# A hand-made order for TensorE in the RWKV stage of a decoder layer

## The chip, the cores and the metric

The kernel runs on one core of a Trainium2 chip. The metric is the device time of one execution in microseconds (us), input to output, and lower is better. One execution was recorded by the hardware profiler; all rows below are from it.

## The reference, cut to what matters

One layer of a decoder, for a prompt of 1024 tokens and 8 sample tokens (1032 columns together). The normed input is projected once, by a wide matrix; the columns of that projection are an RWKV branch, a sliding-window attention, a cross attention and three gates of 1024 columns each:

```python
h = _rmsnorm(x, p['norm_mix'])
proj = h @ p['w_in']
z, q, k, v, xq, gates = jnp.split(proj, IN_SPLITS, axis=-1)
...
out_a, S_new = _rwkv_branch(z, z_prev, S0, p)
...
g = jax.nn.sigmoid(gates)
merged = (g[..., :D_MODEL] * (out_a @ p['w_br_a'])
          + g[..., D_MODEL:2 * D_MODEL] * (out_b @ p['w_br_b'])
          + g[..., 2 * D_MODEL:] * (out_c @ p['w_br_c']))
x = x + merged @ p['w_out']
```

The RWKV branch has 8 heads of 64 and is a recurrence over the tokens, with a state matrix for each head:

```python
sa = jnp.einsum('bhvk,bhk->bhv', S, -kk_t)
S = (S * w_t[:, :, None, :] + sa[..., None] * (kk_t * a_t)[:, :, None, :]
     + v_t[..., None] * k_t[:, :, None, :])
y = jnp.einsum('bhvk,bhk->bhv', S, r_t)
```

The vectors `kk` are normed to length one for each head; `y` is normed, scaled, and multiplied by an output gate.

## The kernel before, in words

**The input projection** is done in pieces of 128 of its columns (`in_proj`): a load of 512 KB (`wst`), a split of the weights into two parts (`wh` on ScalarE, `wl` on GpSimd), and 72 products on TensorE: three column groups (384, 384 and 264 of the 1032 tokens) by 8 blocks of the depth by 3 pairs of parts (L181 to L183, in `dense`). ScalarE then evacuates each group. A gate piece ends in a tanh and a store (L286, L287); an RWKV piece ends in the token shift on VectorE (L348 to L350). There are 48 pieces.

**The RWKV stage** handles the recurrence in 8 units: two groups of four heads by four quarters of the 1024 tokens. Unit u does, in this order:

- first half: loads of z; the decay and `aa` products (L459, L460); a scan (L470); sums of squares by products with `hsel` (L481), an inverse root of some ten small VectorE operations (L122 to L127), L493 and L496, a second `hsel` product (L498); a transpose of the norms, written to memory and read back over all partitions (`bsum`, then `rn`, L506 and L510), for `kk` times `rn` (L512); then `BR` and `CK` (L536 to L539).
- the matrices: 32 products of `CK` and `BR` (L548), masked into `GM` on VectorE (L551). The 32 by 32 diagonal blocks go out to memory (`amat<-GM`, L555) and come back in another layout (`AT<-amat`, L577).
- the loop on VectorE: 31 steps of two operations (L584, L586) solve the small triangular systems. The result goes out (`xmat<-X`, L588) and into `GM` (`GM<-xmat`, L591); a transpose (L593) follows.
- the two inverse steps on TensorE: 16 products (L600) with an evacuation by ScalarE, and 16 more (L603).
- four chunks one after the other, each a chain: state times `BR` (L618), `GM` times `UV` (L627), ScalarE (L630), a product (L634), ScalarE (L635), a product (L637), the new state on VectorE (L640); L642 makes the output of the chunk.
- the end: group norm on VectorE (L660, L661) and ScalarE (L669), transposes (L672), the output gate's products (L680), a store.

The state goes from unit to unit within a group of heads, so chunks of different units of a group can't change places. The pools hold two buffers of `GM`, `BR`, `CKT` and `UV`, one of `AT`.

**What sets the order.** The program is written unit by unit, with pieces of the input projection between (a list `FILL`: RWKV pieces of the second group, and ten gates). A scheduler then orders the instructions of each engine. In what it made, the matrices of unit u + 1 (L548) stand on TensorE ahead of the inverse steps of unit u (L600), and the loop of unit u + 1 on VectorE lies between the state updates (L640) of unit u. Twenty-two pieces lie in the stage; the last four gates are made where the branches are merged, just before the branch projections.

Of the kernel before, what the change touches and what calls it, by code (L numbers as in the profile page):

```python
# [18 lines left out]
P = 128  # L19
# [70 lines left out]
def tile_step(ctx, tc, I, O):  # L90
    nc = tc.nc
    V, A, G, PE, SY = nc.vector, nc.scalar, nc.gpsimd, nc.tensor, nc.sync
    cnt = [0]

# [181 lines left out]

    gate_d = mk(dr, "gate", [24, P, NT])
    todo = list(range(24))

    def gates(n):  # L280
        for _ in range(min(n, len(todo))):
            i = todo.pop(0)

            def evac(g, s, w, b):
                gt = mk(hp, "gt", [P, w], F32, 2)
                op = A.activation(gt, b, AF.Tanh, scale=0.5)  # L286
                SY.dma_start(gate_d[i, :, s:s + w], gt)  # L287
                return op
            in_proj(G0 + i * P, evac)
# [50 lines left out]
    def rw_proj(mt, out):  # L340
# [6 lines left out]
        G.tensor_copy(zl[:, :, mt], z[:, T:T + 9])  # L347
        V.tensor_tensor(out[:, 0:T], z[:, 0:T], z[:, 1:T + 1], ALU.subtract)  # L348
        V.tensor_tensor(out[:, T:NT], shT[:, :, mt], z[:, T + 1:NT + 1], ALU.subtract)
        V.scalar_tensor_tensor(out, out, col(C_MU + mt), z[:, 1:NT + 1], ALU.mult, ALU.add)  # L350
# [80 lines left out]
    def unit(jj, q):  # L431
# [56 lines left out]
        rsqrt(sn[:, 0], sn[:, 2], sn[:, 1])  # L488
        for e in range(2):
# [4 lines left out]
        for e in range(2):  # L494
            for c in spans[e]:
                V.scalar_tensor_tensor(tmp[:, c], zr[:, c], col(C_RK + 2 * jj + e), zk[:, c], ALU.mult, ALU.mult)  # L496
        for i, (c0, w) in enumerate(tl):
            PE.matmul(sb[:w, 1, :, i], lhsT=tmp[:, c0:c0 + w], rhs=hsel, start=True, stop=True)  # L498
        V.tensor_copy(sn[:, 3, :, 0:4], sb[:, 1, :, 0:4])
        if end:  # L500
            V.tensor_copy(sn[0:2 * NS, 3, :, 4], sb[0:2 * NS, 1, :, 4])
        b = sm_bank([20, P])
# [40 lines left out]
        for c4 in range(2):  # L543
# [13 lines left out]
        for x in range(2):  # L557
            xs_ = slice(4 * x, 4 * x + 4)
            G.tensor_tensor(CK[:, xs_].rearrange("p c a t -> p c (a t)"), CK[:, xs_].rearrange("p c a t -> p c (a t)"),
                            gc[:, xs_].unsqueeze(2).to_broadcast([P, 4, P]), ALU.mult)  # L560
        CKT, UV = mk(rp, "CKT", [P, HN, P], F32, 2), mk(rp, "UV", [P, HN, P], F32, 2)
        for x in range(2):
# [3 lines left out]
            A.activation(CKT[:, 4 * x:4 * x + 4], b, AF.Copy)  # L566
        b = sm_bank([P, 4, P])
        for i in range(4):
            PE.transpose(b[:, i], zv[:, i * P:(i + 1) * P], ident)
        for par in range(2):  # L570
            A.activation(UV[64:128].rearrange("p (c e) v -> p c e v", e=2)[:, :, par], b[par * 64:par * 64 + 64], AF.Copy)

# [21 lines left out]
        XP = mk(rp, "Y", [32, 16, 32])  # L594
        for x in range(2):
# [17 lines left out]
        for cc in range(4):  # L613
# [16 lines left out]
            A.activation(pt, pp[0:64], AF.Copy)  # L630
            pz = cp_bank([P, 512])
# [3 lines left out]
            A.activation(UVc[0:64, :, cc], pu, AF.Copy)  # L635
            for e, hh, hs in both:
# [7 lines left out]
            A.activation(Yc[(cc % 2) * 64:(cc % 2) * 64 + 64, :, cc // 2], pp[64:128], AF.Copy)  # L644
        if end:
# [24 lines left out]
        b = cp_bank([P, 4, P])  # L670
# [6 lines left out]
        for s, w, cols in banks:  # L677
            b = cp_bank([P, w])
# [1100 lines left out]
```

## Time and profile before

| what | value |
| --- | --- |
| time, median of 3 runs | 2063.13 us (2058.52 to 2069.75) |
| the profiled execution's own time | 2070.15 us |
| its span, first to last instruction | 2068.2 us |
| TensorE busy | 1928.9 us (93%) |
| VectorE, ScalarE, GpSimd busy | 63%, 38%, 31% |
| TensorE's granted clock over the span | 0.946 of full speed |
| the RWKV stage | 182 to 730 us, TensorE's clock 0.81 to 1.00 by unit |

The profiled execution took 7.0 us more than the median. "Busy" adds up the time of an engine's instructions; a wait inside the pipeline of matrix products also counts as busy.

### The profile page before, as it was taken

Reading aid. Unit: us, or ns where it says so; the run is one execution under the profiler, and the core shown is the slowest. Engines: PE = TensorE matmul, PEld = TensorE weight load, DVE = VectorE, ACT = ScalarE, POOL = GpSimd, SP = SyncE. Lnnn points to the kernel's source line nnn. Section 1 sums busy time; section 2 is a strip of 40 time slices with the busy share of each in tenths; the row PEclk is TensorE's granted clock in tenths of the full one; section 3 lists DMA queues with packets and bytes.
Section 4 is the critical chain, followed back from the end, with each engine's and each line's share of the span. In section 5 each row is a group of like instructions: output and inputs, shape, how many; then the busy total and the mean of one; then the engine's idle time right before and its main releaser. Section 6 shows DMA issues by size and latency. Waiting matters only on the chain. (4 is left out here: it accounts for less than half of the span.)

```text
span 2068.2 us, 36968 instructions
## 1 busy us (share of the span) xinstructions
PE 1928.9 (93%) x14079; PEld 1835.2 (89%) x14079; DVE 1305.7 (63%) x3021; ACT 786.1 (38%) x1701; POOL 643.8 (31%) x706
## 2 busy tenths in 40 slices
PE   5998889989999988999999999979999998999998
PEld 4878777878888978989889999969999998999997
DVE  7545756465565466467742575687665668788864
ACT  5432323433433334345642123343333344344433
POOL 3423212322321144222010000146755644444321
PEclk9999888989999999989989999979999999999999
DMA  4543322333321155233236346416444448455413
GB/s 142 168 156 115 98 52 78 94 93 81 96 81 52 37 160 163 62 92 89 67 114 197 113 144 199 123 43 203 155 149 144 147 151 277 124 149 156 142 39 101
DMA packets 257102, 250.68 MB, mean 121 GB/s; under 512 B 43101, under 2 KB 204958, under 8 KB 256926
## 3 DMA queue, kind: packets, MB, share of 16 engines
q1 hardware_dynamic: 254656, 241.24, 38.3%
q0 software_dynamic: 2016, 6.53, 1.0%
q8 instruction: 111, 1.82, 0.4%
q10 hardware_dynamic: 254, 0.55, 0.1%
q14 instruction: 65, 0.53, 0.1%
HBM read 174.19 MB, written 74.46 MB: 120 GB/s over the span
## 5 line engine op out<-in xcount | busy, mean ns | idle before, releaser
L181 PE MATMUL mm<-hh,wh 128*128 128x384 f32 (+1 forms) x1152 | 390.0, 339 | 5.3 <-ACT z L345 5.0
L182 PE MATMUL mm<-hl,wh 128*128 128x384 f32 (+1 forms) x1152 | 386.9, 336 | 6.9 <-DVE hl L217 6.9
L183 PE MATMUL mm<-hh,wl 128*128 128x384 f32 (+1 forms) x1152 | 384.8, 334 | 1.4 <-POOL wl L174 1.4
L1566 PE MATMUL z<-h,wl 128*128 128x258 f32 x1488 | 266.6, 288 | 10.1 <-ACT wh L1547 3.4
L1566 PE MATMUL z<-h,wh 128*128 128x258 f32 x1488 | 264.8, 286 | 6.6 <-DVE wh L1321 3.6
L182 PEld LDWEIGHTS mm<-hl,wh 128*128 128x128 f32 x1152 | 225.6, 196 | 10.9 <-DVE hl L217 7.7
L181 PEld LDWEIGHTS mm<-hh,wh 128*128 128x128 f32 x1152 | 225.1, 195 | 9.4 <-ACT z L345 5.4
L1566 PEld LDWEIGHTS z<-h,wl 128*128 128x128 f32 x1488 | 218.3, 193 | 12.0 <-ACT wh L1547 3.5
L183 PEld LDWEIGHTS mm<-hh,wl 128*128 128x128 f32 x1152 | 225.3, 196 | 4.0 <-POOL wl L174 1.7
L1566 PEld LDWEIGHTS z<-h,wh 128*128 128x128 f32 x1488 | 217.7, 193 | 7.7 <-DVE wh L1321 3.8
L1659 DVE TENSOR_TENSOR x<-z,x 128x516 f32<-128x516 f32 x168 | 115.6, 689 | 69.2 <-PE z L1566 66.6
L1566 PE MATMUL z<-l,wl 128*128 128x258 f32 x744 | 154.9, 288 | 3.1 <-DVE l L1321 3.1
L1566 PE MATMUL z<-l,wh 128*128 128x258 f32 x744 | 154.3, 287 | 1.2 <-DVE l L1321 1.2
L174 POOL TENSOR_TENSOR wl<-wst,wh 128x1024 fp32r<-128x1024 f32 x48 | 116.8, 2432 | 105.0 <-ACT wh L173 99.6
L173 ACT ACTIVATE wh<-wst 128x1024 fp32r<-128x1024 f32 x84 | 88.8, 1057 | 142.1 <-PE mm L182 73.1
L1566 PEld LDWEIGHTS z<-l,wl 128*128 128x128 f32 x744 | 118.2, 193 | 3.7 <-DVE l L1321 3.6
L1514 POOL TENSOR_TENSOR sw<-wst 128x256 f32<-128x256 f32 (+1 forms) x56 | 55.1, 984 | 211.3 <-DMA wst<-in_w_down 102.3
L1566 PEld LDWEIGHTS z<-l,wh 128*128 128x128 f32 x744 | 118.2, 193 | 1.8 <-DVE l L1321 1.8
L1618 POOL TENSOR_TENSOR us<-us,us 128x516 f32<-128x516 f32 x64 | 96.5, 1519 | 54.0 <-issue 21.8
L1321 DVE TENSOR_TENSOR l<-ub,h 128x516 fp32r<-128x516 f32 (+1 forms) x120 | 92.8, 798 | 6.9 <-ACT h L1346 6.7
L183 PE MATMUL mm<-oh,wl 128*128 128x384 f32 (+1 forms) x288 | 92.2, 320 | 0.0
L182 PE MATMUL mm<-ol,wh 128*128 128x384 f32 (+1 forms) x288 | 92.1, 320 | 0.0
(514 smaller groups left out, 4329.8 us busy)
## 6 DMA issues: line engine op xcount, KB each, us to landing
u<-us SPq DMA_DIRECT2D x112, 258.0 KB
ub<-u SPq DMA_DIRECT2D x112, 258.0 KB
wst<-in_w_in SPq DMA_DIRECT2D x48, 512.0 KB
wst<-in_w_down SPq DMA_DIRECT2D x24, 512.0 KB
gate<-gt SPq DMA_DIRECT2D x48, 192.0 KB
gl<-gate SPq DMA_DIRECT2D x16, 516.0 KB
wst<-in_w_out SPq DMA_DIRECT2D x16, 512.0 KB
wst<-in_w_up SPq DMA_DIRECT2D x16, 512.0 KB
```

Of the source, the lines that this page charges most:

```text
L173: A.activation(hi, st, AF.Copy)
L174: last_lo[:] = [eng.tensor_tensor(lo, st, hi.bitcast(F32), ALU.subtract)]
L181: PE.matmul(out, lhsT=wh, rhs=xh, start=first and k == 0, stop=False)
L182: PE.matmul(out, lhsT=wh, rhs=xl, start=False, stop=False)
L183: end = PE.matmul(out, lhsT=wl, rhs=xh, start=False, stop=last and k == n - 1)
L1321: V.tensor_tensor(lo, x, hi.bitcast(F32), ALU.subtract)
L1514: G.tensor_tensor(s[:, k:k + n], v, w, op)
L1566: op = PE.matmul(z[:, s, :HQ], lhsT=t[:, a, k], rhs=right[ks[k], s, i][b], start=go and k + q == 0, stop=q == 2 and k == nk - 1, skip_grou ...
L1618: G.tensor_tensor(t, x, y, ALU.subtract)
L1659: V.tensor_tensor(c, z, c, ALU.add)
```

## The change

TensorE's products and transposes of the stage now go through a small class that keeps them in program order. A unit is cut into more than 20 steps by `yield`; the main program calls the steps, and `fill(us)` puts input projection products between them, counted at 0.45 ns for each column. The matrices of unit u + 1 are called after the third chunk of unit u. The scratch tile of the inverse steps, `XP`, moves from the tag `Y` to the tag `AT`; the last transposes and output products take another bank of PSUM. Sixteen gates (before: twelve) and all of the other 10 pieces are products of `fill` in this stage, and no gate is left for the merge. The other engines are ordered by the scheduler, as before.

```diff
+    class Products:
+        traced = False
+        def kept(self, op):
+            return tc.keep_in_program_order(op) if self.traced else op
+        def matmul(self, *a, **k):
+            return self.kept(nc.tensor.matmul(*a, **k))
...
+    def filling():
+        while pieces:
+            c0, begin = pieces.pop(0)
+            evac, finish = begin()
+            w = pre.pop(c0, None) or wpiece(w_in[:, :, c0:c0 + P], KT, P, eng=G)
+            if pieces and pieces[0][0] not in pre:
...
+                n0 = pieces[0][0]
+                pre[n0] = wpiece(w_in[:, :, n0:n0 + P], KT, P, eng=G)
+            for g, (s, n) in enumerate(GR):
+                b = mm_bank([P, n])
+                for k in range(KT):
+                    for q, (x, y) in enumerate(((0, 0), (0, 1), (1, 0))):
+                        PE.matmul(b, lhsT=w[x][:, k], rhs=h[g][y][:, k], start=k + q == 0, stop=k == KT - 1 and q == 2)
+                        if g < 2 or k < KT - 1 or q < 2:
+                            yield n
...
+    def fill(us):
+        nonlocal filler
+        while us > 0:
+            n = next(filler, None)
...
+            us -= n * 0.00045
...
         V.transpose(XW[0:32], gm[0:32, :, 0:32])
-        XP = mk(rp, "Y", [32, 16, 32])
+        XP = mk(ra, "AT", [P, NT])[0:32, 0:512].rearrange("p (m t) -> p m t", t=32)
...
-        b = cp_bank([P, 4, P])
+        yield
+        b = sm_bank([P, 4, P])
         for i in range(4):
             PE.transpose(b[:, i], Y[:, i], ident)
...
-    FILL = [lambda: pair_proj(2), lambda: pair_proj(3)] + [lambda i=i: gates((2, 2, 2, 2, 2)[i]) for i in range(5)]
-    next(units[0])
-    next(units[0])
-    for u in range(7):
-        next(units[u + 1])
-        if u == 0:
-            FILL[0]()
-        flush(units[u])
-        next(units[u + 1])
-        if u:
-            FILL[u]()
+    def begin(u):
+        if u < 8:
+            step(u)
+            fill(1.0)
+            step(u)
+            fill(1.0)
+    def matrices(u):
+        step(u)
+        fill(0.8)
+        step(u)
+    def turned(u):
+        step(u)
+        fill(0.8)
+        step(u)
+    def chunks(u):
+        for cc in range(4):
+            for us in (0.65, 0.65, 1.0):
+                step(u)
+                fill(us)
+            if cc == 2 and u < 7:
+                matrices(u + 1)
+                fill(0.6)
+    def lead(u):
+        step(u)
+        fill(1.6)
+        step(u - 1)
+        fill(0.6)
+        step(u)
+        step(u + 1)
...
+    gate_pieces(14)
+    PE.traced = True
+    begin(0)
+    step(0)
+    fill(6.0)
+    step(0)
+    fill(0.5)
+    step(0)
+    fill(10.0)
+    matrices(0)
+    fill(1.6)
+    turned(0)
+    for u in range(8):
+        begin(u + 1)
+        step(u)
+        step(u + 1)
+        step(u - 1)
+        fill(9.0 if 0 < u < 7 else 16.0)
+        step(u + 1)
+        fill(0.5)
+        lead(u)
+        if u < 7:
+            chunks(u)
+            turned(u + 1)
+    PE.traced = False
...
-    gates(1)
-    heads = [xhead(0)]
-    flush(prev)
-    heads += [xhead(hd) for hd in range(1, 4)]
-    gates(1)
+    heads = []
+    gate_pieces(1)
+    for hd in range(4):
+        pieces.append((X0 + hd * P, lambda hd=hd: xparts(hd)))
+    gate_pieces(1)
+    PE.traced = True
+    chunks(7)
+    step(7)
+    fill(6.0)
+    step(7)
+    PE.traced = False
+    for _ in filler:
+        pass
```

In the changed program every product stands at L103 and every transpose at L106 (inside the class). L638 there is L551 of before, L668 is L575, L677 and L679 are L584 and L586, L599 is L512, L601 is L514, L625 is L538, L736 is L640.

TensorE before, near the end of the stage: the matrices of one unit (`BR_5256`, `CK_5257`) and the inverse steps of the unit ahead of it (`GM_4847`).

```order
L548 MATMUL sm_5476<-BR_5256,CK_5257 128x128 x3
L548 MATMUL sm_5475<-BR_5256,CK_5257 128x128
L548 MATMUL sm_5476<-BR_5256,CK_5257 128x128
L565 MATMUL sm_5493<-c_ident_69,CK_5257 128x128 x4
...
L600 MATMUL cp_5267<-GM_4847,XW_4897 64x64 x8
...
L569 MATMUL sm_5505<-c_ident_69,zv_5178 128x128 x4
L603 MATMUL cp_5278<-Y_5266,XW_4897 64x64 x8
L618 MATMUL cp_5290<-st_127_601,BR_4641 128x128 x2
```

TensorE in the change, at the same kind of place: the end of the third chunk of unit 2 (`GM_3126`), projection products (`mm`), and the matrices of unit 3 (`BR_3662`).

```order
L103 MATMUL cp_3793<-UV_3221,CKT_3220 64x64 x4
L103 MATMUL cp_3777<-UV_3221,GM_3126 64x64 x4
L103 MATMUL mm_3773<-hh_4_75,wl_3535 128x384
...
L103 MATMUL sm_3821<-BR_3662,CK_3663 128x128
L103 MATMUL sm_3822<-BR_3662,CK_3663 128x128
...
L103 MATMUL mm_3859<-hl_7_78,wh_3534 128x384
L103 MATMUL cp_3862<-st_126_600,BR_2977 128x128 x2
```

The matrices of the next unit have moved from ahead of the inverse steps to behind three of the four chunks; only the fourth chunk follows them before the next unit's inverse steps.

VectorE before, within the loop of a unit: the state update of the unit ahead of it (L640) stands between the loop's operations.

```order
L586 TENSOR_TENSOR X_4901<-X_4901,xt_4930 128x3x22
L584 TENSOR_TENSOR xt_4933<-X_4901,AT_4899 128x63
L640 TENSOR_TENSOR st_128_602<-dS_4736,cp_4745 64x2x64 x2
L586 TENSOR_TENSOR X_4901<-X_4901,xt_4933 128x3x21
L584 TENSOR_TENSOR xt_4936<-X_4901,AT_4899 128x60
```

VectorE in the change, from the end of the loop of unit 2 (`X_3342`) to the beginning of that of unit 3 (`X_4007`).

```order
L679 TENSOR_TENSOR X_3342<-X_3342,xt_3434 128x8
...
L599 TENSOR_TENSOR kk_3300<-kk_3300,rn_3636 128x528
L601 SCALAR_TENSOR_TENSOR aa_3256<-aa_3256,kk_3300 128x528
...
L736 TENSOR_TENSOR st_126_600<-dS_3672,cp_3685 64x2x64 x2
L736 TENSOR_TENSOR st_125_599<-dS_3721,cp_3736 64x2x64 x2
...
L736 TENSOR_TENSOR st_126_600<-dS_3780,cp_3793 64x2x64 x2
L638 TENSOR_TENSOR GM_3820<-sm_3821,gmask_574 128x4x128
...
L736 TENSOR_TENSOR st_125_599<-dS_3865,cp_3878 64x2x64 x2
...
L677 TENSOR_TENSOR xt_4009<-X_4007,AT_4005 128x31
```

No state update stands inside a loop any more: the four of a unit lie between two loops. In this unit, and in unit 6, the multiplication by `rn` (L599), which waits for a transfer, stands ahead of the first of them; in unit 0 behind the first, elsewhere behind the second. Inside the loops of units 0 to 6 stand instead the next unit's inverse root, L493, L496 and L539 (by their lines of before).

## Rows read from the trace of the kernel before

**Rows 1.** Windows: each engine's busy us (instructions), TensorE clock, DMA share, GB/s.
```profile
182.00:278.90 96.90, 77.75 (x466) 72.22 (x465) 60.72 (x150) 29.25 (x57) 25.71 (x36) 0.86 0.33 96
663.40:730.20 66.80, 65.11 (x514) 61.00 (x514) 26.46 (x100) 24.19 (x52) 11.08 (x17) 1.00 0.15 45
1073.20:1119.80 46.60, 46.26 (x299) 45.91 (x298) 6.85 (x6) 14.08 (x25) 7.21 (x3) 1.00 0.74 237
```

**Rows 2.** Timeline of TensorE: start, us, instruction, [idle before it and its releaser].
```profile
278.91 1.97 PE L600 MATMUL cp<-GM,XW 32*64 32x64 f32 x16 [5.48 <-DMA GM<-xmat]
...
285.83 1.22 PE L618 MATMUL cp<-st,BR 128*128 128x128 f32 x4
...
605.28 3.10 PE L548 MATMUL sm<-BR,CK 64*128 64x128 f32 x32
...
629.67 1.19 PE L618 MATMUL cp<-st,BR 128*128 128x128 f32 x4 [4.30 <-DVE st L640]
...
663.36 1.14 PE L600 MATMUL cp<-GM,XW 32*64 32x64 f32 x16
...
666.57 0.71 PE L618 MATMUL cp<-st,BR 128*128 128x128 f32 x4
...
671.53 0.61 PE L618 MATMUL cp<-st,BR 128*128 128x128 f32 x4
```

**Rows 3.** Timeline of the sync engine's DMA issues: start, issue time, instruction.
```profile
211.60 0.87 SPq L555 DMA_DIRECT2D amat<-GM  x2
...
214.67 0.62 SPq L577 DMA_DIRECT2D AT<-amat  x1
...
276.46 0.85 SPq L591 DMA_DIRECT2D GM<-xmat  x2
...
468.80 1.14 SPq L510 DMA_DIRECT2D rn<-bsum  x2
...
556.86 0.57 SPq L577 DMA_DIRECT2D AT<-amat  x1
...
609.73 0.97 SPq L555 DMA_DIRECT2D amat<-GM  x2
...
616.36 0.55 SPq L577 DMA_DIRECT2D AT<-amat  x1
...
652.24 0.55 SPq L588 DMA_DIRECT2D xmat<-X  x1
...
657.05 0.86 SPq L591 DMA_DIRECT2D GM<-xmat  x2
```

**Rows 4.** Timeline of VectorE, columns as in rows 2.
```profile
473.84 0.69 DVE L512 TENSOR_TENSOR kk<-kk,rn 128x512 f32<-128x512 f32 x1
...
565.76 0.24 DVE L584 TENSOR_TENSOR xt<-X,AT 128x31 f32<-128x31 f32 x1 [0.28 <-DMA AT<-amat]
...
626.63 0.19 DVE L584 TENSOR_TENSOR xt<-X,AT 128x31 f32<-128x31 f32 x1 [6.93 <-DMA AT<-amat]
```

**Rows 5.** Groups of VectorE by line, 182 to 730 us: busy, mean ns, idle.
```profile
L586 DVE TENSOR_TENSOR X<-X,xt 128x60 f32<-128x60 f32 (+24 forms) x248 | 66.5, 268 | 5.4
...
L584 DVE TENSOR_TENSOR xt<-X,AT 128x60 f32<-128x60 f32 (+24 forms) x248 | 62.5, 252 | 43.9 <-DMA AT<-amat 27.4 <-POOL X L579 11.2
...
L496 DVE SCALAR_TENSOR_TENSOR tmp<-zr,pv,zk 128x256 f32<-128x256 f32 (+1 forms) x20 | 8.5, 426 | 0.0
...
L493 DVE TENSOR_TENSOR zk<-zk,tmp 128x512 f32<-128x512 f32 (+1 forms) x8 | 5.5, 691 | 3.1 <-ACT tmp L492 3.1
...
L125 DVE TENSOR_TENSOR sn<-sn 128x10 f32<-128x10 f32 x24 | 3.9, 162 | 0.1
```

**Rows 6.** Windows after two idle times of TensorE, columns as in rows 1.
```profile
276.10:296.60 20.50, 16.53 (x96) 13.99 (x96) 16.27 (x49) 3.00 (x8) 3.76 (x6) 0.50 0.31 84
629.67:636.67 7.00, 7.00 (x42) 5.67 (x42) 3.50 (x21) 0.76 (x2) 0.72 (x2) 0.50 0.00 0
```

**Rows 7.** The second window of rows 1, products with tile wh alone.
```profile
663.40:730.20 66.80, 44.57 (x183) 31.15 (x184) 0.00 (x0) 3.18 (x3) 7.15 (x3) 1.00 0.15 45
```

More of the change, by code (lines that the diff above doesn't have):

```diff
@@ L274, in tile_step, with gate_evac, evac @@
     start.close()
+    pieces = []
+    def filling():
[4 more added lines that the diff above has]
+            if pieces and pieces[0][0] not in pre:
+                if not hold and evs[1] is not None:
+                    hold.append((evs[1],))
+                n0 = pieces[0][0]
[7 more added lines that the diff above has]
+                            yield n
+                        else:
+                            last_n = n
+                op = evac(g, s, n, b)
+            evs[:] = evs[1], op
+            finish()
+            yield last_n
+    filler = filling()
+    def fill(us):
+        nonlocal filler
+        while us > 0:
+            n = next(filler, None)
+            if n is None:
+                if not pieces:
+                    return
+                filler = filling()
+                continue
+            us -= n * 0.00045
     gate_d = mk(dr, "gate", [24, P, NT])
     todo = list(range(24))
+    def gate_evac(i):
+        def evac(g, s, w, b):
+            gt = mk(hp, "gt", [P, w], F32, 2)
+            op = A.activation(gt, b, AF.Tanh, scale=0.5)
+            SY.dma_start(gate_d[i, :, s:s + w], gt)
+            return op
+        return evac
     def gates(n):
@@ L282, in gates, with gate_pieces @@
             i = todo.pop(0)
[L284 to L289, printed above, removed]
+            in_proj(G0 + i * P, gate_evac(i))
+    def gate_pieces(n):
+        for _ in range(n):
+            i = todo.pop(0)
+            pieces.append((G0 + i * P, lambda i=i: (gate_evac(i), lambda: None)))
     oa_d = mk(dr, "oa", [4, P, NT])
@@ L338, in tile_step, with rw_parts @@
             G.memset(states[j][i], 0.0)
-    def rw_proj(mt, out):
+    def rw_parts(mt, out):
         z = mk(ra, "z", [P, NT + 1])
@@ L345, in evac, with finish, rw_proj, pair_pieces @@
             return A.activation(z[:, 1 + s:1 + s + n], b, AF.Copy)
-        in_proj(mt * P, evac)
[L347 to L350, printed above, removed]
+        def finish():
+            G.tensor_copy(zl[:, :, mt], z[:, T:T + 9])
+            V.tensor_tensor(out[:, 0:T], z[:, 0:T], z[:, 1:T + 1], ALU.subtract)
+            V.tensor_tensor(out[:, T:NT], shT[:, :, mt], z[:, T + 1:NT + 1], ALU.subtract)
+            V.scalar_tensor_tensor(out, out, col(C_MU + mt), z[:, 1:NT + 1], ALU.mult, ALU.add)
+        return evac, finish
+    def rw_proj(mt, out):
+        evac, finish = rw_parts(mt, out)
+        in_proj(mt * P, evac)
+        finish()
+    def pair_pieces(j):
+        def begin(mt):
+            zs = mk(ra, "zso", [P, NT])
+            evac, mix = rw_parts(mt, zs)
+            def finish():
+                mix()
+                SY.dma_start(zs_d[mt], zs)
+            return evac, finish
+        for mt in (4 + j, j, 8 + j):
+            pieces.append((mt * P, lambda mt=mt: begin(mt)))
     wd = mk(ra, "AT", [P, NT])
@@ L697, in tile_step, with step @@
     units = [unit(jj, q) for jj in range(2) for q in range(4)]
-    FILL = [lambda: pair_proj(2), lambda: pair_proj(3)] + [lambda i=i: gates((2, 2, 2, 2, 2)[i]) for i in range(5)]
-    next(units[0])
-    next(units[0])
-    for u in range(7):
-        next(units[u + 1])
-        if u == 0:
-            FILL[0]()
-        flush(units[u])
-        next(units[u + 1])
-        if u:
-            FILL[u]()
+    def step(u):
+        if 0 <= u < 8:
+            next(units[u], None)
+    def begin(u):
[27 more added lines that the diff above has]
+        step(u + 1)
+    for j in (2, 3):
+        pair_pieces(j)
+    gate_pieces(14)
[23 more added lines that the diff above has]
+    PE.traced = False
     prev = units[7]
```

53 lines of the change are left out of this document (36 added, 17 removed).

## The prediction

> **What bounds the kernel now.** I looked at windows of the span first. In the stage from 182 to 278.9 us TensorE is busy for 77.75 of 96.9 us, in the last part, from 663.4 to 730.2, for 65.11 of 66.8, and at the merge, from 1073.2 to 1119.8, for 46.26 of 46.6 [rows 1]. So TensorE is nearly full except where the first unit starts: time goes away when a product goes away, or when an idle gap closes, and time comes in when a gap opens. Then I read the timeline of TensorE for the place where a unit begins to use its results, the inverse steps L600. Unit 0 reaches it at 278.91, after 5.48 us of idle that a transfer (GM<-xmat) ended; unit 7 reaches it at 663.36 [rows 2]. Seven periods take 384.45 us, 54.9 us each. That number is what the change has to beat. The third view is the sync engine's transfers [rows 3] with the timeline of VectorE [rows 4]: they show what a unit needs from its matrices L548 to its L600, whatever the other engines do.
>
> **The chain from L548 to L600, row by row.** Matrices to the issue of the write of the blocks: 605.28 [rows 2] to 609.73 [rows 3], 4.45 us. Write to issue of the load of AT: 211.60 to 214.67, 3.07 us (6.63 in unit 7, where other transfers are ahead in the queue) [rows 3]. Load to the loop's first operation: 556.86 [rows 3] to 565.76 [rows 4], 8.90 us, nearly all of it the transfer, since VectorE idled 0.28 us for it at the end; in unit 7 616.36 to 626.63, 10.27 us, with 6.93 us of idle. The loop: 31 times (0.268 + 0.252), 16.1 us [rows 5]. The way back: 652.24 to 657.05, 4.81 us, and 276.46 to 278.91, 2.45 us [rows 2, 3]. The sum is 39.8 us without any disturbance. Before, this runs beside the chunks of the unit ahead of it, since L548 of unit u + 1 stands ahead of L600 of unit u; it is stretched by state updates in the loop, but hidden.
>
> **What the order does.** In the change L548 of unit u + 1 comes after the third chunk of unit u. So from one L600 to the next, two legs stand one behind the other.
>
> First leg, L548 to L600: the 39.8 us, and what stands in the loop of VectorE. There the next unit's first half has been put: L493 (0.691 us), two of L496 (0.426 each), L539 (of L493's shape), and about ten small operations of the inverse root (0.162 each) [rows 5]: 0.69 + 0.85 + 0.69 + 1.62 = 3.9 us. That makes 43.7. TensorE's own work in this leg is one chunk and the fills of about 16 us in the code (0.8, 0.6, 2.3, 0.8, 2.0, 9.0, 0.5), some 25 us with the unit's small products, so it idles for 43.7 - 25 = 19 us there.
>
> Second leg, L600 to the next L548: in unit 7, 663.36 to the first chunk at 666.57 is 3.21 us, and a chunk is 671.53 - 666.57 = 4.96 us [rows 2], three of them 14.9: 18.1. The fills inside a chunk lie in its waits for ScalarE and VectorE; the fill of 1.6 and 0.6 us and the last products of the unit ahead, between L600 and L603, do not all: 2.4 is an estimate from the fills and half hidden products. 20.5 us.
>
> Two further terms. The norms are transposed after L600 in the pinned order, and `kk` needs their way through memory: a write and a load like xmat's, 4.81, and then rn from 468.80 to 473.84, 5.04 us [rows 3, 4]. Where VectorE has that multiplication ahead of the first state update (two units), the update, wanted some 4 us after the first chunk starts, comes about 7 us late, and everything on TensorE behind it; in unit 0 2.5: 16.5 / 7 = 2.4 us for each period. The others hide it behind the second chunk.
>
> And the clock. [...] I take 3.5; the bounds are 0 and 7.4 (a chunk at the lower level too).
>
> Period: 43.7 + 20.5 + 2.4 + 3.5 = 70.1 us, 15.2 over 54.9.
>
> **The sum, for the profiled execution of 2070.15 us.**
>
> - Start: unit 0's blocks go out at 211.60 as before [rows 3]; then 3.07 + 8.90 + 16.1 + 6.6 (the block of unit 1 and one token shift in the loop, an estimate from the 3.9 above) + 4.81 + 2.45 gives an L600 at 253.5 instead of 278.91: -25 us. Nothing of unit u - 1 stands in its way there. Bounds -30 and 0.
> - Seven periods: 7 x 15.2 = +106 us. The bounds: with the loop alone (16.1), no clock loss and no late `rn`, 39.8 + 20.5 = 60.3, +38; with 10.27 for the load, 7.4 for the clock and a loop mixed as above, 75.4, +143.
> - After the last L600: before, 183 products on `wh` in the window [rows 7], two of three products, so 274 in all, 3.8 pieces of 72. In the change's order 6.0 pieces follow. Four pieces take 46.6 us at the merge [rows 1], 11.65 each: 2.2 x 11.65 = +26 us.
> - The merge: four gates are gone from there, -46.6 us [rows 1]. The DMA share in that window is 0.74, for transfers that run ahead under them (the branch outputs, gates and weights for the merge); with the cover gone they cost at worst 0.74 x 46.6 = 34 us, at best nothing. Most of them can be issued earlier, so I take 7: -40 us. Bounds -47 and -13.
>
> -25 + 106 + 26 - 40 = +67 us: 2137 us for this execution. It is 7.0 us over the median of the runs, so **2130 us** in the median; on its own this case goes from 2095 to 2170. The move of XP costs nothing: the load of the next AT comes after the chunks, long after L603. The bank of the output products costs nothing either as long as the matrices come first in it.
>
> [...] The 512 KB load of AT took 8.9 to 10.3 us where GM<-xmat took 2.45 [rows 3, 4]. [...]
>
> **Rivals.**
>
> - A, faster: TensorE's filled order is the bound and the chain hides behind it. The products of a period, 25 us of fill and 19 of the unit's own (estimates from the code and the chunk's row), with small waits make 50 us: -25 - 34 + 26 - 40 = -73, 1990 us. For it: TensorE is the engine that is full in [rows 1], and no state update interrupts the loop any more. Against it: the first leg must then be done within 28 us, and the load of AT and the loop alone are 25.
> - R, a quick load: on a quieter queue the AT load lands like GM<-xmat, 2.45 instead of 8.90 us, in every unit. Period 63.6, start 6 less: -31 + 61 + 26 - 40 = +16, 2079 us. Against it: in unit 5 as in unit 7 the row is 9 to 10 us.
> - B, no change: only the bare legs, period 60.3: -25 + 38 + 26 - 40 = -1, 2062 us. The point from which the change loses is about 60.5 us for each period.
> - C, slower still: the lower clock lasts through the first chunks of each unit as in unit 0, where 0.50 held for 20.5 us [rows 6], and the loads are slow as in unit 7: 75.4 and 1 for fills at that clock, 76.4: -25 + 150 + 26 - 40 = +111, 2174 us. [...]
> - D, the pins don't bind. The order shows that they do.
>
> **How the numbers follow.** Chances: forecast 0.50, R 0.05, A 0.15, B 0.12, C 0.15, D 0.03 (at 2063). A measurement of this kernel can't tell less than about 0.5% (10 us) from no change. A gives faster 0.15; B, with its spread of 20 us to either side, gives 0.04 of faster, 0.05 of same and 0.03 of slower; D and the low edge of R and the forecast give same another 0.05; the rest is slower: 0.19, 0.10, 0.71. The range leaves out A and the upper part of C, about 0.2: 2045 to 2185.
>
> **What would show it.** In the profile after: L548 of a unit starting some 20 us after L600 of the unit ahead; TensorE idle for 10 to 20 us ahead of each L600, ended by GM<-xmat or by the evacuation chain from it; the loop on VectorE without state updates, 20 us long; periods of about 70 us; granted clock near 0.5 behind each L600; L600 of unit 0 near 254; about 94 us after the last L600; no gate at the merge and small waits for loads there. I am wrong if the first leg is done in under 35 us (an AT load of 3 us would show it), if TensorE does not idle ahead of L600, or if the periods are 60 us or less.

## The result, and the profile after

The changed kernel takes 2212.71 us in the median of 4 runs (2207.13 to 2219.32), the kernel before 2061.34 in the same comparison: the ratio is 1.0728, with an interval of 1.0684 to 1.0772. It was forecast slower, at 2130 us and at most 2185; it is slower by more than twice the forecast amount (151 us for 67). The span of the profiled execution went from 2068.2 to 2211.3 us, 143.1 more, where the sum said 67.

First the windows of the changed kernel, with columns as in [rows 1]: the start, the two legs of one period (unit 3's inverse steps to the matrices of unit 4, and from there to the inverse steps of unit 4), the first leg behind unit 6's inverse steps, the part after the last inverse steps, and the merge.

```profile
182.00:254.46 72.46, 54.23 (x356) 51.10 (x355) 49.44 (x124) 20.46 (x40) 20.22 (x26) 0.90 0.35 105
497.83:522.97 25.14, 25.14 (x212) 22.00 (x213) 8.27 (x23) 8.57 (x21) 6.10 (x10) 0.90 0.26 73
522.97:572.20 49.23, 28.44 (x219) 25.91 (x218) 29.98 (x110) 14.88 (x33) 9.99 (x13) 0.81 0.31 76
720.22:762.72 42.50, 31.47 (x211) 27.06 (x211) 7.05 (x23) 7.29 (x18) 7.91 (x11) 0.67 0.14 44
810.73:905.00 94.27, 94.27 (x654) 89.26 (x655) 29.68 (x104) 30.78 (x63) 16.41 (x21) 0.91 0.15 43
1240.00:1280.00 40.00, 22.47 (x135) 21.34 (x134) 12.14 (x17) 9.98 (x18) 0.00 (x0) 0.79 0.68 230
```

Read the TensorE column against the length of each stretch. From the inverse steps to the next matrices TensorE is busy all the time (25.14 of 25.14). From the matrices to the next inverse steps it is busy for 28.44 of 49.23 us. Behind unit 6 the first kind of stretch lasts 42.50 us in place of 25.14, at a clock of 0.67.

The timeline of TensorE in the changed kernel, with columns as in [rows 2]:

```profile
254.46 1.97 PE L103 MATMUL cp<-GM,XW 32*64 32x64 f32 x16 [16.97 <-DMA GM<-xmat]
...
497.83 1.97 PE L103 MATMUL cp<-GM,XW 32*64 32x64 f32 x16 [17.00 <-DMA GM<-xmat]
...
506.17 0.61 PE L103 MATMUL cp<-st,BR 128*128 128x128 f32 x4
...
511.79 0.61 PE L103 MATMUL cp<-st,BR 128*128 128x128 f32 x4
...
522.97 1.16 PE L103 MATMUL sm<-BR,CK 64*128 64x128 f32 x16
...
572.20 1.96 PE L103 MATMUL cp<-GM,XW 32*64 32x64 f32 x16 [20.79 <-DMA GM<-xmat]
...
741.18 0.45 PE L106 MATMUL sm<-c_ident,sv 128*96 128x128 f32 x1 [11.03 <-POOL sv L606]
741.42 1.06 PE L103 MATMUL cp<-st,BR 128*128 128x128 f32 x4
...
751.22 0.92 PE L103 MATMUL cp<-st,BR 128*128 128x128 f32 x4
...
810.73 1.93 PE L103 MATMUL cp<-GM,XW 32*64 32x64 f32 x16 [26.62 <-DMA GM<-xmat]
```

The products `cp<-GM,XW` are the inverse steps. Each of these waits for GM<-xmat, after 17 to 27 us of idle (13.7 in units 2 and 6). They start at 254.46 in unit 0 (278.91 before) and at 810.73 in unit 7 (663.36 before): seven periods of (810.73 - 254.46) / 7 = 79.5 us, where [rows 2] gives 54.9 and the forecast was 70.1. A chunk takes 511.79 - 506.17 = 5.62 us. Ahead of unit 6's chunks a transpose of `sv` held TensorE for 11.03 us, and the chunk behind it took 9.80 us.

The waits of TensorE in that stage, one row for what most of them waited for (us in all, times, longest):

```profile
PE cp L103 <- DMA GM<-xmat: 151.5, 8, 26.6
```

And the way of unit 4 from its matrices on, by the sync engine's issues and the loop on VectorE:

```profile
527.87 0.96 SPq L644 DMA_DIRECT2D amat<-GM  x2
...
533.87 0.58 SPq L670 DMA_DIRECT2D AT<-amat  x1
...
544.54 0.19 DVE L677 TENSOR_TENSOR xt<-X,AT 128x31 f32<-128x31 f32 x1 [3.66 <-DMA AT<-amat]
...
564.79 0.58 SPq L681 DMA_DIRECT2D xmat<-X  x1
...
569.57 0.86 SPq L684 DMA_DIRECT2D GM<-xmat  x2
```

Matrices at 522.97, write at 527.87 (4.90), load at 533.87 (6.00), first operation at 544.54 (10.67), end of the loop and write at 564.79 (20.25), read at 569.57 (4.78), inverse steps at 572.20 (2.63): 49.2 us. Link by link this is the forecast's chain; the load of AT (8.90 in the forecast) and its issue (3.07) are well longer, the other links within half a microsecond.

At the merge one wait is new:

```profile
PE mm L103 <- ACT wh L188: 16.3, 1, 16.3
```

TensorE waits 16.3 us for the first branch weights, whose loads and split lay under the four gates before.

### The profile page after: what moved, and what is told of

Read it like the earlier page. It is cut to its first block, busy times and chain, and to the rows that moved or that the text cites. A ratio compares the mean times of both kernels' runs of the same rounds, so it can differ in the third digit from the quotient of the medians.

```text
span 2211.3 us, 36977 instructions
## 1 busy us (share of the span) xinstructions
PE 1920.5 (87%) x14079; PEld 1831.3 (83%) x14079; DVE 1316.3 (60%) x3021; ACT 788.2 (36%) x1701; POOL 647.7 (29%) x706
## 5 line engine op out<-in xcount | busy, mean ns | idle before, releaser
L103 PE MATMUL mm<-hh,wh 128*128 128x384 f32 (+1 forms) x1152 | 393.6, 342 | 6.2 <-ACT z L409 5.0
L103 PE MATMUL mm<-hl,wh 128*128 128x384 f32 (+1 forms) x1152 | 391.2, 340 | 7.3 <-DVE hl L232 7.3
L103 PE MATMUL mm<-hh,wl 128*128 128x384 f32 (+1 forms) x1152 | 389.6, 338 | 1.3 <-POOL wl L189 1.3
L103 PE MATMUL z<-h,wl 128*128 128x258 f32 x1488 | 266.4, 288 | 9.7 <-DVE x L1827 5.6
L103 PE MATMUL z<-h,wh 128*128 128x258 f32 x1488 | 262.2, 284 | 7.9 <-DVE wh L1489 4.9
L103 PEld LDWEIGHTS mm<-hl,wh 128*128 128x128 f32 x1152 | 229.4, 199 | 12.1 <-DVE hl L232 8.1
L103 PEld LDWEIGHTS mm<-hh,wh 128*128 128x128 f32 x1152 | 229.3, 199 | 11.6 <-ACT z L409 5.5
L103 PEld LDWEIGHTS mm<-hh,wl 128*128 128x128 f32 x1152 | 229.4, 199 | 5.5 <-POOL wl L189 1.7
L103 PEld LDWEIGHTS z<-h,wl 128*128 128x128 f32 x1488 | 218.3, 193 | 11.2 <-ACT wh L1715 3.0
L103 PEld LDWEIGHTS z<-h,wh 128*128 128x128 f32 x1488 | 215.2, 191 | 9.0 <-DVE wh L1489 5.1
L103 PE MATMUL z<-l,wl 128*128 128x258 f32 x744 | 154.8, 288 | 3.1 <-DVE l L1489 3.1
L103 PE MATMUL z<-l,wh 128*128 128x258 f32 x744 | 152.9, 285 | 1.0 <-DVE l L1489 0.9
L103 PE MATMUL cp<-GM,XW 32*64 32x64 f32 x128 | 15.7, 312 | 151.5 <-DMA GM<-xmat 151.5
L103 PEld LDWEIGHTS cp<-GM,XW 32*64 32x64 f32 x128 | 14.2, 219 | 153.7 <-DMA GM<-xmat 126.9
L103 PEld LDWEIGHTS z<-l,wl 128*128 128x128 f32 x744 | 118.2, 193 | 3.7 <-DVE l L1489 3.6
L103 PEld LDWEIGHTS z<-l,wh 128*128 128x128 f32 x744 | 116.7, 191 | 1.7 <-DVE l L1489 1.7
L1786 POOL TENSOR_TENSOR us<-us,us 128x516 f32<-128x516 f32 x64 | 96.7, 1521 | 54.9 <-issue 23.8
L103 PE MATMUL mm<-oh,wh 128*128 128x384 f32 (+1 forms) x288 | 93.0, 323 | 16.3 <-ACT wh L188 16.3
```

The lines of the kernel that those rows point to most:

```text
L103: return self.kept(nc.tensor.matmul(*a, **k))
L1786: G.tensor_tensor(t, x, y, ALU.subtract)
```

## The experiments

The theory: the matrices of the next unit stand behind the third chunk, so two legs, matrices to inverse steps (48 us) and inverse steps to matrices (31 us), follow one another in each period. Rivals: the pins or the fills themselves cost the time; the lower clock does; single late instructions do.

| run | edit | median us | ratio to before, interval |
| --- | --- | --- | --- |
| changed kernel | | 2212.71 | 1.0728, 1.0684 to 1.0772 |
| e1_early | matrices ahead of the inverse steps, pinned | 2092.50 | 1.0132, 1.0094 to 1.0170 |
| e2_unpinned | no pins | 2106.80 | 1.0211, 1.0159 to 1.0262 |
| e3_fill2 | 42 us of fills moved to the end | 2244.17 | 1.0852, 1.0809 to 1.0894 |
| e4_at_split | AT load in four DMAs | 2212.19 | 1.0711, 1.0674 to 1.0748 |
| e5_sv_late | transpose of sv two chunks later | 2200.47 | 1.0634, 1.0597 to 1.0671 |
| e6_outer32 | AT load with outermost dimension 32 | 2187.26 | 1.0571, 1.0526 to 1.0616 |
| e7_gates | before, four gates moved | 2080.65 | 1.0062, 1.0031 to 1.0093 |
| e8_before_outer32 | before, with e6's load | 2073.82 | 1.0015, 0.9986 to 1.0044 |
| e9_warm | 80 useless products for each unit | 2208.80 | 1.0676, 1.0656 to 1.0696 |
| e14_warm_full | as many as each idle time holds | 2185.96 | 1.0590, 1.0553 to 1.0627 |
| e10_early2 | matrices behind the inverse steps, ahead of the chunks | 2158.82 | 1.0427, 1.0405 to 1.0450 |
| e11_early2_gates10 | the same, four gates back at the merge | 2188.87 | 1.0578, 1.0559 to 1.0597 |
| e12_early_outer32 | e1, e6's load, sv late | 2076.15 | 1.0041, 1.0021 to 1.0061 |
| e13_early_ahead | e12, first half called ahead | 2074.94 | 1.0045, 1.0023 to 1.0067 |
| e15_norms_first | e13, fills behind the norms' transpose | 2070.58 | 1.0007, 0.9988 to 1.0025 |

Each ratio is to runs of the kernel before made beside that run; its median there lay between 2061.3 and 2070.2 us, so a difference of two medians from different rows is uncertain by some 9 us. By the ratios (in parts of 2063 us) e1 is 123 us below the changed kernel, e5 19, e6 32, e9 11 and e14 28, and e3 26 above it, each give or take some 10 us; the texts below give the medians.

**Where the matrices stand: e1_early, e2_unpinned.** All products stay pinned in e1; the call of the next unit's matrices moves, and with it the norms' transpose, the transpose of `sv` (a step of its own, as in e5), the order of the steps around the inverse steps, and `XP` back to tag `Y`.

```diff
-            if cc == 2 and u < 7:
-                matrices(u + 1)
...
-        fill(9.0 if 0 < u < 7 else 16.0)
+        fill(3.0 if 0 < u < 7 else 10.0)
         step(u + 1)
-        fill(0.5)
+        fill(1.5)
+        step(u + 1)
+        fill(5.0)
+        step(u + 1)
+        if u < 7:
+            matrices(u + 1)
+            fill(0.6)
         lead(u)
```

> The changed kernel, still pinned and with the same fill in each period, but the matrices of unit u + 1 stand ahead of the inverse steps of unit u again (the norms' transpose is called earlier for that, the scratch tile XP is back in tag Y). Serial-chain theory: the leg from the matrices to the inverse steps (48 us in the changed kernel) runs beside the chunks again, so the period falls from 79.5 to 52 to 60 us and the time from 2212 to 2040 to 2090 us. Rival, the pinned order itself or its fills cost the time: the period stays over 70 us, the time over 2150 us.

Measured: 2092.5 us, with a period of (686.80 - 260.21) / 7 = 60.9 us; both lie just over the expected ranges and far under the rival's. In e1 the first leg even lasts 67 to 84 us in units 1 to 6, but it lies beside the chunks. Its timeline at the inverse steps of units 0, 3 (with the matrices of unit 4 ahead) and 7:

```profile
260.21 1.14 PE L103 MATMUL cp<-GM,XW 32*64 32x64 f32 x16
...
439.71 2.08 PE L103 MATMUL sm<-BR,CK 64*128 64x128 f32 x16 [5.78 <-DVE CK L627]
443.56 2.08 PE L103 MATMUL sm<-BR,CK 64*128 64x128 f32 x16
...
448.73 1.14 PE L103 MATMUL cp<-GM,XW 32*64 32x64 f32 x16
...
686.80 1.11 PE L103 MATMUL cp<-GM,XW 32*64 32x64 f32 x16 [3.54 <-DMA GM<-xmat]
```

The inverse steps of units 0 to 6 have no idle time ahead of them any more, those of unit 7 have 3.54 us. They take 1.14 us for all 16, as in unit 7 of [rows 2], where the changed kernel took 1.97. What TensorE waits for now is CK, in six units:

```profile
PE sm L103 <- DVE CK L627: 25.1, 6, 7.5
```

So the place of the matrices, with what moved along with it, is worth 120 of the 151 us (e5, which moves `sv` alone, gives 12); the pins are not the cost.

In e2 the class hands products on without pinning them (`PE.traced = False` in both places).

> The changed kernel with the same program text, TensorE's products not pinned, so the scheduler orders them. The scheduler leaves the matrices of the next unit ahead of or between the inverse steps in units 0, 1, 3 and 5 only in part, elsewhere behind the first chunks. Serial-chain theory: the period lies between that of before and that of the change, 60 to 75 us, time 2080 to 2180 us. Rival, the pins alone are the cost: back to 2060 us or less.

Measured: 2106.8 us, with a period of (719.03 - 253.57) / 7 = 66.5 us. The scheduler, with the same program text, puts 12 to 20 of the 32 products of the next matrices ahead of the inverse steps in units 1, 3 and 5, and all of them among the first chunks elsewhere. This fits the theory and goes against pins as the only cost, which would have given back all; e1, with its pins, is the faster of the two.

**Are the fills in the way, or is TensorE's idle time free? e3_fill2, e9_warm.**

```diff
-        fill(9.0 if 0 < u < 7 else 16.0)
+        fill(2.0 if 0 < u < 7 else 16.0)
```

> The changed kernel with 7 us less of projection products in each of six periods (fill 2.0 in place of 9.0 between a unit's first half and its inverse steps); they are made after the last unit instead. Serial-chain theory: these products lay in TensorE's idle time, so the inverse steps of unit 7 start within 10 us of 810.7 as before, and the 42 us come on top at the end: 2245 to 2260 us. Rival, the fills stand in the chain's way: inverse steps of unit 7 some 42 us earlier, total unchanged near 2212 us.

Measured: 2244.17 us, 31 more than the changed kernel. The inverse steps of unit 7 begin at 797.84 and not at 810.73:

```profile
797.84 1.93 PE L103 MATMUL cp<-GM,XW 32*64 32x64 f32 x16 [16.51 <-DVE XW L686]
```

That is 12.9 us earlier (1.1 of them in the start), where fills on the path would have given 42. So about 29 of the 42 us, two thirds, lay in idle time, and the other 13 came off the path. 12.9 is a little over the 10 us of the expectation. The traced execution, 2231.79 us, is the quickest of the four.

e9 does the opposite and adds 640 products that nothing reads (110 us by an estimate: in e14, at a granted clock of 1.00, products of this shape start 0.17 us apart) ahead of the inverse steps:

```diff
+    def spin(n):
+        b = mm_bank([P, GR[0][1]])
+        for i in range(n):
+            PE.matmul(b, lhsT=wh[:, i % 2, 0:P], rhs=h[0][0][:, i % KT], start=True, stop=True)
...
+        spin(80)
         lead(u)
```

> The changed kernel with 80 useless products of 384 columns (13.8 us at full clock) put on TensorE ahead of the inverse steps of each unit; nothing reads them. Theory of the clock: they lie in the 14 to 19 us in which TensorE idles there, so the inverse steps begin at the upper clock level, the stretch from them to the first chunk falls from 9.2 to about 5.6 us, and the time by 7 times 3.6 us or a little more: 2185 us (2170 to 2195). Rival, the lower clock costs nothing on the path, or comes back with the small products anyway: 2207 to 2225 us.

Measured: 2208.8 us. 110 us of added work cost nothing, which shows the idle time better than a view of waits can. The time is in the rival's range, but on the clock it says little: in six units 3 to 12 us of idle are left ahead of the inverse steps.

**The lower clock: e14_warm_full.** The same with 98, 136, 80, 98, 120, 110, 80 and 150 products.

> As the run with 80 useless products, with as many for each unit as its idle time ahead of the inverse steps holds (98, 136, 80, 98, 120, 110, 80 and 150). Theory of the clock: every unit now begins its inverse steps at the upper level, L600 to the first chunk falls from 9.2 to 6.2 us in units 1, 3, 4 and 5, the period by about 3 us: 2185 to 2200 us. Rival, the lower clock costs under 1 us on the path: 2205 to 2215 us.

Measured: 2185.96 us, 27 below the changed kernel; the two traced executions, 2197.39 and 2213.39 us, are 16 apart. Unit 1 in the changed kernel, from its inverse steps to its first chunk, in a window and the timeline:

```profile
338.53:348.00 9.47, 9.47 (x55) 8.71 (x56) 2.08 (x5) 0.76 (x3) 0.00 (x0) 0.62 0.01 2
338.53 1.97 PE L103 MATMUL cp<-GM,XW 32*64 32x64 f32 x16 [23.65 <-DMA GM<-xmat]
...
348.00 0.61 PE L103 MATMUL cp<-st,BR 128*128 128x128 f32 x4
```

And with the useless products:

```profile
340.97:347.18 6.21, 6.21 (x56) 5.69 (x56) 1.88 (x5) 0.76 (x3) 0.00 (x0) 1.00 0.01 3
340.97 1.14 PE L103 MATMUL cp<-GM,XW 32*64 32x64 f32 x16 [0.17 <-DMA GM<-xmat]
...
347.18 0.61 PE L103 MATMUL cp<-st,BR 128*128 128x128 f32 x4
```

The granted clock of the stretch goes from 0.62 to 1.00 and its length from 9.47 to 6.21 us. The clock term, forecast at 3.5 us, is 3.3 here. In units 3, 4 and 5 it is 2.2, 2.5 and 3.5 (8.34 to 6.18, 9.16 to 6.63 and 9.70 to 6.22), where the granted clock of the changed kernel is 0.71, 0.69 and 0.61; in unit 5 it is 1.00 here (637.62 to 643.84). A product of the inverse steps takes 217 ns in the median, for 309 in the changed kernel. The second legs of all seven periods get 2.8 us shorter on average, the first legs none.

**The load of AT: e4_at_split, e6_outer32, e8_before_outer32.** e4 loads 32 partitions at a time:

```diff
-        SY.dma_start(AT, a_d[u].rearrange("m k s t -> (m k) s t").unsqueeze(0).to_broadcast([4, 32, 32, 32]))
+        for c in range(4):
+            SY.dma_start(AT[32 * c:32 * c + 32], a_d[u].rearrange("m k s t -> (m k) s t"))
```

> The changed kernel with the 512 KB load of AT (outermost dimension: four broadcast copies) split into four loads of 32 partitions each. Serial-chain theory with the load on the path: if each part lands like GM<-xmat (2.6 us) after three more issues of 0.6 us, the load's 10.4 us become about 5, 5.4 us less in each of 8 units: 2170 us. Rival, the bytes or the queue set the 10.4 us: no gain, with 1.8 us more for issues in each unit 2212 to 2227 us.

Measured: 2212.19 us. The time could not tell the two apart. In most units the four DMAs don't stand together in the sync engine's queue; in unit 1 three of them are issued over 5 us after the first, behind another load:

```profile
299.50 0.31 SPq L671 DMA_DIRECT2D AT<-amat  x1
304.49 0.38 SPq L533 DMA_DIRECT2D zv<-zs  x1
304.92 1.38 SPq L671 DMA_DIRECT2D AT<-amat  x3
```

In unit 7 alone the four are issued together, and there the loop begins 6.74 us after the first issue, where the changed kernel takes 9.98:

```profile
785.57 1.85 SPq L671 DMA_DIRECT2D AT<-amat  x4
792.31 0.19 DVE L678 TENSOR_TENSOR xt<-X,AT 128x31 f32<-128x31 f32 x1 [5.09 <-DMA AT<-amat]
```

So the bytes alone don't set the 10 us.

e6 keeps one DMA and renumbers the partitions of AT and X, so that each of 32 rows is followed by its four copies:

```diff
-            xinit[p, c, 4 * c + p // 32] = 1.0
+            xinit[p, c, 4 * c + p % 4] = 1.0
...
-        SY.dma_start(AT, a_d[u].rearrange("m k s t -> (m k) s t").unsqueeze(0).to_broadcast([4, 32, 32, 32]))
+        SY.dma_start(AT, a_d[u].rearrange("m k s t -> (m k) s t").unsqueeze(1).to_broadcast([32, 4, 32, 32]))
...
-        SY.dma_start(x_d[u].rearrange("m k (c q) t -> q (m k) c t", q=4), X)
+        for qq in range(4):
+            SY.dma_start(x_d[u].rearrange("m k (c q) t -> q (m k) c t", q=4)[qq], X[qq::4])
```

> The changed kernel with partitions of AT and X numbered so that the one load of AT has an outermost dimension of 32 and not of 4 (four copies of each of 32 rows); the write of X becomes four DMAs, three more issues of 0.6 us. Theory, a transfer with few outermost entries is slow: the load falls from 10.4 to 4 to 5 us, 4 us less in each of 8 units after the issues, on the path: about 2180 us. Rival, its bytes or the queue set its time: no gain and 1.7 us more in each unit, 2212 to 2226 us.

Measured: 2187.26 us, 25 less. The load of unit 7 in the changed kernel:

```profile
775.62 0.57 SPq L670 DMA_DIRECT2D AT<-amat  x1
785.60 0.19 DVE L677 TENSOR_TENSOR xt<-X,AT 128x31 f32<-128x31 f32 x1 [8.31 <-DMA AT<-amat]
```

and in e6:

```profile
760.42 0.57 SPq L670 DMA_DIRECT2D AT<-amat  x1
765.26 0.19 DVE L677 TENSOR_TENSOR xt<-X,AT 128x31 f32<-128x31 f32 x1 [3.18 <-DMA AT<-amat]
```

9.98 us against 4.84, with the same 512 KB. Why the one is slower was not shown. In six of the eight units VectorE is at other work until after the load has landed (its loop begins without a wait), so the gain is 25 us and not the 41 of eight such loads. A part of it is the write of X, whose outermost dimension changed too: from its first issue to that of GM<-xmat it takes 3.9 to 4.1 us, with four issues, where the changed kernel takes 4.8 to 5.2 with one.

> The kernel before with the AT load of outermost dimension 32 and X written in four DMAs. Theory: in the kernel before the chain from matrices to inverse steps lies beside the chunks, so a quicker load saves at most the part of the first unit, 0 to 10 us: 2054 to 2066 us. Rival, the chain bounds that kernel too: 2030 us or less.

The same edit in the kernel before gives 2073.82 us, over the expected range, but beside a kernel before that took 2070.0 there: 1.0015 of it (0.9986 to 1.0044), no difference. The load is quicker there as well (unit 7: 627.41 to 632.65, 5.24 us for the 10.27 of before), but the chain is beside the chunks.

**One late instruction: e5_sv_late.** A step of its own begins at the transpose of `sv` and is called after the second chunk.

```diff
             G.tensor_scalar(sv[:, :, 5], aa[:, W:n].rearrange("p (j n) -> p j n", j=2), 0.5, None, op0=ALU.mult)
+        yield
+        if end:
             b = sm_bank([12 * NS, P])
             PE.transpose(b, sv.rearrange("p e a b -> p (e a b)"), ident)
...
+            if cc == 1:
+                step(u + 1)
             if cc == 2 and u < 7:
                 matrices(u + 1)
```

> The changed kernel with one TensorE instruction moved: the transpose of sv, which exists in units 3 and 7 alone and waits for the norms' way through memory, and what follows it up to BR and CK, are called after the second chunk instead of ahead of the first. Theory: that transpose is what holds TensorE for 11 us ahead of the chunks of units 2 and 6, and the lower clock behind it costs another 4 us in the first chunk: 29 us in all, 2183 us (2175 to 2195). Rival, VectorE's order (the multiplication by rn ahead of the first state update) holds the chunks anyway, or the matrices of the next unit wait instead: 2200 us or more.

Measured: 2200.47 us, 12 less, 29 expected; it is at the edge of the rival's range. The stretch from inverse steps to chunks fell as it should in unit 2, from 18.3 us (413.16 to 431.43) to 9.7 (413.92 to 423.61), but the transpose still waits behind the second chunk:

```profile
413.92 1.96 PE L103 MATMUL cp<-GM,XW 32*64 32x64 f32 x16 [13.76 <-DMA GM<-xmat]
...
423.61 0.61 PE L103 MATMUL cp<-st,BR 128*128 128x128 f32 x4
...
439.95 0.45 PE L106 MATMUL sm<-c_ident,sv 128*96 128x128 f32 x1 [4.95 <-POOL sv L606]
440.19 1.06 PE L103 MATMUL cp<-st,BR 128*128 128x128 f32 x4
```

and the first products of the chunk behind it take 1.06 us again where 0.61 is usual; in the changed kernel the chunk that began with 1.06 us had a granted clock of 0.50 (431.43 to 441.16). From inverse steps to the next matrices unit 2 takes 35.65 us for 39.39 and unit 6 31.94 for 42.50: 14 us less in the two. So in unit 2 most of the wait only moved, in unit 6 most of it went. `sv` needs the norms from memory, and in unit 2 it is ready later than two chunks take. The rival's first half, VectorE's order, is not tested apart: with this edit the multiplication by `rn` also went behind the second state update.

**The gates alone: e7_gates.** The kernel before with `gates(5)` for the last `gates(1)` of the stage, so that none is left for the merge.

> The kernel before with one edit: four more gates at the end of the RWKV stage, none at the merge. Theory: TensorE is full in both places, so the four gates cost some 45 us at the one and give back 32 to 40 us at the other: within 15 us of before, 2055 to 2075 us. Rival, the gates fill gaps of the stage: 2020 to 2040 us.

Measured: 2080.65 us, 6 over the expected range, 1.0062 of before: the four gates cost a little more in the stage than they give back at the merge.

**Versions that were to beat both kernels.** e10 places the matrices of the next unit behind the inverse steps and ahead of the chunks, with the norms' transpose ahead of the inverse steps.

```diff
-        fill(9.0 if 0 < u < 7 else 16.0)
+        fill(2.0 if 0 < u < 7 else 12.0)
         step(u + 1)
         fill(0.5)
+        step(u + 1)
         lead(u)
+        fill(6.5)
+        if u < 7:
+            matrices(u + 1)
+            fill(0.6)
```

> The pinned order with the matrices of the next unit ahead of the chunks, and with what held TensorE in the first such version taken away: the norms are transposed ahead of the inverse steps of the unit before and the matrices follow those, with fills between, so the way of the norms through memory is covered; the transpose of sv follows the matrices. Fourteen gates as fill. Theory: the 25 us of waits for CK and 14 for sv go, period 53 us and less: 2020 to 2065 us. Rival, other waits take their place: 2080 us or more.

Measured: 2158.82 us. The expectation was wrong by its own theory: from inverse steps to the next matrices is still a leg, 11 to 16 us, and it comes on top of the other.

```profile
470.31 1.96 PE L103 MATMUL cp<-GM,XW 32*64 32x64 f32 x16 [8.42 <-DMA GM<-xmat]
...
483.73 1.16 PE L103 MATMUL sm<-BR,CK 64*128 64x128 f32 x16
...
543.05 1.96 PE L103 MATMUL cp<-GM,XW 32*64 32x64 f32 x16 [11.37 <-DMA GM<-xmat]
```

13.4 and 59.3 make this period of 72.7 us (70.7 on average). This separates "ahead of the inverse steps" (e1) from "ahead of the chunks" (e10).

> The same with ten gates in the stage in place of fourteen and four left at the merge as in the kernel before, and smaller fills within the chunks. Theory: a gate costs TensorE the same in the stage as at the merge, so within 15 us of the version with fourteen, on the lower side because transfers at the merge keep their cover: 2015 to 2060 us. Rival, the stage needs these products as cover: slower than the version with fourteen by over 15 us.

e11, with ten gates in the stage and fills of 0.45, 0.45 and 0.6 us in the chunks, took 2188.87 us, 30 more than e10, as the rival had it. Its period is (753.93 - 254.11) / 7 = 71.4 us, no shorter than e10's: in a stage that waits, less work in the waits gives nothing, and the gates at the merge cost time.

e12 is e1 with e6's load and the transpose of sv behind the matrices; e13 also calls `turned(u + 1)` ahead of the chunks and the first half of unit u + 2 within them; e15 has fills of 0.6, 1.0 and 10.0 us around the `hsel` product and the norms' transpose in place of e13's 5.0, 1.5 and 5.0.

> The pinned order with the matrices of the next unit ahead of the inverse steps, with the AT load of outermost dimension 32, and the transpose of sv behind the matrices. Theory: in that order the period of 60 us is a chain too (end of a loop, norms through memory, matrices, AT, loop), so a load that is 5 us quicker and no wait for sv make it 54 to 56 us: 2050 to 2070 us. Rival, TensorE's own products bound it there: 2085 us or more.

> The same, and the first half of the unit after the next is called within the chunks, right after the transposes of CK of the next unit, so the norms are ready earlier. Theory: the chain of e12 gets shorter by several us for each unit, until TensorE with its fills bounds it: 2030 to 2060 us. Rival, VectorE takes the added work ahead of state updates and the chunks get longer: no faster than e12.

> The version with early matrices and the first half called ahead, with the fills moved behind the norms' transpose (0.6, 1.0 and 10.0 us in place of 5.0, 1.5 and 5.0), so that the norms' way through memory is covered. Theory: there TensorE waited 44 us for CK ahead of the matrices in eight units; with the transpose some 5 us earlier most of it goes: 2035 to 2055 us, a little below both kernels. Rival, the wait moves on to the loop or to AT: 2065 us or more.

Measured: 2076.15, 2074.94 and 2070.58 us, ratios of 1.0041, 1.0045 and 1.0007. All three missed their ranges; for e13 and e15 the rivals came true (no faster than e12; the wait moves on). TensorE's waits for CK and for GM<-xmat, in e13 and then in e15:

```profile
PE sm L103 <- DVE CK L620: 43.9, 8, 8.0
...
PE cp L103 <- DMA GM<-xmat: 3.0, 1, 3.0
```

```profile
PE sm L103 <- DVE CK L620: 15.5, 7, 3.9
PE cp L103 <- DMA GM<-xmat: 14.6, 2, 8.4
```

28 us less waiting for CK gave 4 to 8 us in time (by the medians and by the ratios); 12 us of it came back as waits for GM<-xmat. The best pinned order is as fast as the kernel before; none beats it.

## Why the prediction was wrong in size

The step that failed is the term of seven periods: +106 us forecast, 7 x (79.5 - 54.9) = +172 measured. The mechanism, two legs one behind the other, was right (e1, e3 and e9 show it); both legs were sized too short, the first by 4.6 us for each period (32 in all), the second by 4.8 (34).

- **First leg**, forecast 43.7, measured 48.3 on average over units 1 to 7 (45.3 to 51.8). Where the rows had two values for a link, I took the shorter. AT's load lasted 10.0 to 10.9 us (8.90 taken, though 10.27 stood in the same rows), the issue of that load 2.4 to 8.2 us after the write (3.07 taken), the loop with its guests 17 to 27 us, 21.5 on average (20.0 taken). 10.27 and the middle of 3.07 and 6.63 would have given 46.9. Most of the rest is the loop: in unit 1 it holds two token shifts and two scans besides the guests that I counted (26.7 us).
- **Second leg**, forecast 20.5 + 2.4 + 3.5 = 26.4, measured 31.2. In units 1, 3, 4 and 5, where nothing is late, it is 25.1 to 26.7 us for 24.0: a chunk takes 5.6 us and not 4.96, so the fills in it are not wholly hidden. With the smaller fills of e11 a chunk takes 4.8 us (567.76 to 572.56), in e10, with the fills of the change, 5.5. In units 2 and 6 the leg is 39.4 and 42.5 us, some 13 and 17 over these four units, where I had 7 each: the late `rn` was foreseen, but put on VectorE's order. That order is there, but the chunk has not begun: it is TensorE's own transpose of `sv`, pinned ahead of the chunks and itself in need of `rn`, that waits 8 to 11 us, and the chunk behind it takes 9.73 and 9.80 us at a granted clock of 0.50, for 5.6 at 1.00. e5 shows both parts in unit 2, though there the wait comes back two chunks later. Unit 0, at 32.3, waits once for a token shift ahead of its state update.
- **The clock term** was about right: 3.5 forecast, 2.2 to 3.5 in units 1, 3, 4 and 5 by e14, 2.8 on average over the seven second legs. No run shows the 3.5 us as it was taken, nor its bound of 7.4: both were estimates. What the runs show is a granted clock of 0.61 to 0.71 over the 8.34 to 9.70 us from the inverse steps to the first chunk in these four units, and of 1.00 in e14 over 6.21 us in unit 1 and 6.22 in unit 5.
- **The start** was right: inverse steps of unit 0 at 254.46 for 253.5. There is some luck in it: the load took 9.98 us for 8.90, the loop 22.0 for 22.7.
- **After the last inverse steps**: 94.27 us for 92.8.
- **The merge**: -32 us for -40 (from 730.2 to the span's end 1338.0 us before, from 905.0 1306.3 now). The lost cover is one wait of 16.3 us, not 7. e7 agrees that moved gates gain nothing.
- **The rivals**: C, slower still, was nearest, with 2174 us, and half for its own reason. Its slow load was there in every unit; its clock that stays low through the chunks was not: the chunks of units 1, 3, 4 and 5 ran at 1.00, and only single chunks of units 0, 2 and 6, behind a further wait, at 0.51, 0.50 and 0.50, and unit 7's first at 0.51. A and B needed legs that the rows did not allow. R, a quick load, is not what the kernel has, but e6 came near it (4.84 us in unit 7, where R had 2.45), and found 25 us where R's sum of 51 had the gain in every unit. (The row that R gives to unit 5 is unit 6's.)

Not settled: why the period of e15, (666.15 - 263.11) / 7 = 57.6 us, stays over the 54.9 of before, and whether another pinned order would be faster. That was not tried.

## What to carry to other kernels

When an order is fixed by hand, find the longest chain that one unit starts and another unit ends, and see whether its first instruction still stands ahead of the work that is to cover it; here one place, behind three chunks and not ahead of the inverse steps, with what moved along, was worth 120 us of 151. Add up such a chain from typical rows, not from the quicker row of a link, and look on TensorE itself for every pinned instruction that waits for memory, as the transpose of `sv` did for 8.16 and 11.03 us. Useless products put into an idle time show cheaply whether it is free, and what the clock behind it costs: here 110 us of them cost nothing in e9, and in e14 27 us came back.

## What the runs showed of the hardware that was not expected

A transfer of 512 KB went from 9.98 to 4.84 us (unit 7) when its outermost dimension went from 4 to 32, with the same bytes, both issued by the sync engine; the forecast had counted 8.90 us for it. And 16 to 27 us could be had from products that compute nothing: in units 1 and 5 TensorE's granted clock was 1.00 with them from the inverse steps to the first chunk (6.21 and 6.22 us), and 0.62 and 0.61 over 9.47 and 9.70 us without them, behind idle times of 23.65 and 19.04 us.
